# Part of the second head pair's key projection moved into the first stage of an encoder layer

## The chip, the cores and the metric

The kernel runs on one core of one Trainium2 chip. The metric is the device time of one execution in microseconds (us): shorter is better. The engines are named as in the profile: PE (TensorE, matrix multiplications and transposes), PEld (its weight loads), DVE (VectorE), ACT (ScalarE), POOL (GpSimd) and SP (SyncE, which issues the DMAs). Each engine works through its own list of instructions in order.

## What is computed

One encoder layer over 2048 tokens of width 1024, all in float32:

```
mod = silu(c) @ ada_w + ada_b                     # shift, scale, gate
h = layernorm(x) * (1 + scale) + shift
proj = h @ w_in                                   # 9216 columns
q_h, i_h, zf_fw, zf_bw, g_h, q_n, k_n, v_n, g_n = split(proj)
y_hg = bidirectional gated recurrence(q_h, i_h, zf_fw, zf_bw, g_h)
y_na = neighbourhood attention(q_n, k_n, v_n) * silu(g_n)   # 16 heads of 64
y = concat(y_hg, y_na) @ w_out
out = layernorm(2**0.25 * x + gate * y) * ln_g + ln_b
```

The change is in the projection `h @ w_in` for the keys of the attention.

## The kernel before

**Tokens and columns.** The kernel handles the tokens in two halves of 1024, and a half in two groups `g` of 512. `h` is kept transposed: 8 tiles `k` (128 of the 1024 channels each) of 128x512 for each group, every one of them as two float32r tiles, a rounded one and the remainder: `hts[g, k, 0]` (high) and `hts[g, k, 1]` (low). A weight is split the same way. A column tile is 128 columns of `w_in`; its projection for one group is 8 steps `k` of three matmuls each (weight high by h high, weight high by h low, weight low by h high), 24 matmuls of 128x512 that add up in one PSUM bank. `proj_mm` makes one step of three (L278). `evac` copies the bank out with ACT (L766) into a tile of the tag `raw`, which in this stage is one of eight buffers `e`.

**First stage** (`startup`, about the first 98 us). It normalizes the first 1024 tokens, computes shift and scale, and turns `x` into `h`, step by step over the list `order`: (0, 0) to (0, 7) for the first 512 tokens, then (1, 0) to (1, 7) for the second 512. For each step, PE does four transposes (`turn_`, L232), ACT adds scale and shift (L237) and makes the high part (L239), DVE the low part (L1211). Then `proj_mm` uses the step for three column tiles at once: keys, queries and gates of the attention's first head pair (PSUM banks `acc`). I call these nine matmuls a block. Behind each block `next(values)` does one step of the value projection (`vproj`, L291, twelve matmuls of 128x256; after its last step the copies L297). The turns run one step ahead: the loop body first issues the jobs of the step, then `turn_`, `high` and `low` of the next step, then the block. `jobs` puts the rest between: weight splits, `mod_sum` (a multiply and sum on DVE, L154, which gives shift and scale of one `k`), and for the second tokens `stat` (L202), `rates` (L180 to L209, with ACT's L182 and L183) and `scale` (ACT's L225 and DVE's L227, on `x` in place). For PE, SP, ACT and DVE the stage's instructions stand in the order in which the program writes them.

**The stream behind it.** `first_half` then goes through the eight head pairs of the attention for these 1024 tokens. While pair `w` is attended to (`natten_woven`: scores L1029 and L1036, softmax on DVE and ACT with L1045 to L1055, turns L1078, sums L1100), `first_stream` projects keys, queries and gates of pair `w + 1`, and `weave` mixes the two on PE by a table of costs: a step of three matmuls counts `KUS` = 0.68. Here only PE's order is the program's; a scheduler places the instructions of the others, and it also lets some of this stage's instructions into the end of the first stage (`Prep.k`, L966 to L968: copies of the keys into `KA`, `KB` and `KL`). Weights for the stream come through `Chunks`: `load` issues a DMA into one of four `wraw` buffers, `split` makes the two float32r tiles with ACT (L817) and DVE (L818).

`ps("po")` gives one of two PSUM banks, `tl("ada", ...)` one of four buffers of 128x2048, in which the modulation weights are loaded.

Of the kernel before, what the change touches and what calls it, by code (L numbers as in the profile page):

```python
# [11 lines left out]
F32R = mybir.dt.float32r  # L12
# [5 lines left out]
D = 1024  # L18
# [20 lines left out]
def body(ctx: ExitStack, tc: tile.TileContext, t):  # L39
# [234 lines left out]
    def proj_mm(pz, his, los, g, k):  # L274
        wh = his[k // 4][:, (k % 4) * P:(k % 4 + 1) * P]
        wl = los[k // 4][:, (k % 4) * P:(k % 4 + 1) * P]
        for n, (a, b) in enumerate(((wh, hts[g, k, 0]), (wh, hts[g, k, 1]), (wl, hts[g, k, 0]))):
            pe.matmul(pz, a, b, start=(k == 0 and n == 0), stop=(k == KT - 1 and n == 2))  # L278

    def vproj(src, dst, half, feed=None, fine=False):  # L280
        his, los = feed.take(4) if feed else load_split(lambda i: src[:, i * 512:(i + 1) * 512], 4)
        for t2 in range(2):
            pzs = [ps("pj"), ps("pj")]
            for k in range(KT):
                wh, wl = (w[k // 2][:, (k % 2) * 256:(k % 2 + 1) * 256] for w in (his, los))
                for tp in range(2):
                    for i in range(2):
                        g, o = divmod(((t2 * 2 + tp) * 2 + i) * P, GRP)
                        hh, hl = (hts[g, k, s][:, o:o + P] for s in range(2))
                        for n, (a, b) in enumerate(((hh, wh), (hh, wl), (hl, wh))):  # L290
                            pe.matmul(pzs[tp][:, i * 256:(i + 1) * 256], a, b, start=(k == 0 and n == 0 and i == 0), stop=(k == KT - 1 and n == 2), skip_group_check=True)  # L291
                if k % 2:
                    if k == KT - 1:
                        for tp, pz in enumerate(pzs):
                            v = tl("vo")
                            with tc.high_priority(offset=PRI):
                                act.activation(v, pz, AF.Copy)  # L297
# [553 lines left out]
    def first_stream(st, feed):  # L851

        if st.p % 2 == 0:
            for _ in vproj(t["w_v"][st.p // 2], nv_d[st.p // 2], 0, feed):
                feed.tick()
                yield 2.9
        todo = []
        for n, c in NCOL0:
            his, los = feed.take(2)
            for g in range(2):  # L860
                pz = ps("pj")
                for k in range(KT):
# [311 lines left out]
    def startup():  # L1174
# [29 lines left out]
        def turn_(g, k):  # L1204
            pts[g, k] = h_turn(xs[g], k)

        def high(g, k):
            tmps[g, k] = h_high(pts[g, k], k, hts[g, k, 0], True)

        def low(g, k):  # L1210
            dve.tensor_tensor(hts[g, k, 1], tmps[g, k], hts[g, k, 0], op=ALU.subtract)  # L1211
# [10 lines left out]
        for i in range(4):  # L1222
# [9 lines left out]
            (0, 3): [(mod_sum, 4), (w_split, 1, 1), (w_split, 2, 1)],  # L1232
            (0, 4): [(feed.split, 0), (mod_sum, 5)],
            (0, 5): [(mod_sum, 6), (stat, 1, 0), (feed.split, 0)],
            (0, 6): [(mod_sum, 7), (stat, 1, 1)],
            (0, 7): [(stat, 1, 2), (stat, 1, 3), (rates, 1), (scale, 1, 0, 2)],
            (1, 2): [(scale, 1, 1, 4)],
        }
# [8 lines left out]
        values = vproj(t["w_v"][0], nv_d[0], 0, feed, True)  # L1247
        rows = {n: [None, None] for n, _ in NCOL0}
        order = [(g, k) for g in range(2) for k in range(KT)]
        turn_(0, 0)  # L1250
        high(0, 0)
        w_split(0, 0)
        low(0, 0)
        for n, (g, k) in enumerate(order):
            for f, *a in jobs.get((g, k), []):
                f(*a)
            nxt = order[n + 1] if n + 1 < len(order) else None
            if nxt:
                turn_(*nxt)
            if nxt:  # L1260
                high(*nxt)
                low(*nxt)
            if (g, k) == (0, 7):
                feed.load(8)
                rp = bias_rows()
                bias_fill()
                dma(lg, t["lb_logits"])
                dma(normg, t["hg_norm_g"])
            if (g, k) == (1, 0):
                acc.update({(2, 1): ps("po"), (0, 1): ps("sc"), (1, 1): ps("sc")})  # L1270
                bias_tables(rp)
                bias_pair(0)
                dma(c_d.rearrange("(p k) -> p k", k=KT), mod["c8"])
            for i in (2, 0, 1) if g else (0, 1, 2):
                proj_mm(acc[i, g], *ws[i], g, k)
            if k == KT - 1:
                for i in range(3):
                    rows[NCOL0[i][0]][g] = evac(acc[i, g])
            next(values, None)
            if g:  # L1280
                feed.tick()
        return rows, feed

    def first_half(raws, feed):

        st = Prep(0, 0, raws)
        for n, g in (("k", 0), ("k", 1), ("q", 0), ("g", 0), ("q", 1), ("g", 1)):
# [90 lines left out]
    h_alloc()  # L1378
    with psum_phase("n0", NPS), tc.manual_schedule(engines={mybir.EngineType.PE}):
        with phase("st", SB_, SMS), tc.manual_schedule(engines={getattr(mybir.EngineType, e) for e in ("PE", "SP", "Activation", "DVE")}):  # L1380
            raws, feed = startup()
        with phase("n0", NB0, SM0):
            natten_init(4, 0)
            st = first_half(raws, feed)

    def reload(g):
        for k in range(KT):
# [251 lines left out]
```

## Time and profile before

| | us |
|---|---|
| median of 3 runs | 2625.78 (2624.72 to 2625.88) |
| profiled execution, its own time | 2628.06 |
| profiled execution, span of its instructions | 2626.3 |
| PE busy | 2562.5 (98%) |
| PEld busy | 2149.1 (82%) |
| DVE busy | 1738.8 (66%) |
| ACT busy | 1434.5 (55%) |

A timeline row reads: start, duration, engine, source line, operation, output<-input, count, and in brackets the idle time of the engine before it with what ended it. A row of stages reads: from:to, length, then busy us (and instructions) of PE, PEld, DVE, ACT and POOL, the granted TensorE clock as a share of the full one, the busy share of the DMA engines, and GB/s. Ends of matmuls are modelled; their starts are the better guide.

### The profile page before, as it was taken

What the parts mean: (1) busy time and instruction counts of PE and PEld (TensorE: products, weight loads), DVE (VectorE), ACT (ScalarE), POOL (GpSimd) and SP (SyncE); (2) the same over time, 40 slices, a digit from 0 to 9 for tenths busy, and PEclk for the clock granted to TensorE, in tenths of its full rate; (3) what the DMA queues carried; (4) which work ended last, traced back from release to release, by engine and by line L of the source; (5) the groups of instructions that cost most, each with busy time, mean ns of one, the idle gap of its engine ahead of it and who ended that gap; (6) DMA issues with size and microseconds to landing.
All of it is one profiled execution on the core that took longest, in us unless ns stands there. A gap on an engine that the chain in (4) does not pass through costs nothing.

```text
span 2626.3 us, 45803 instructions
## 1 busy us (share of the span) xinstructions
PE 2562.5 (98%) x17140; PEld 2149.1 (82%) x17140; DVE 1738.8 (66%) x4354; ACT 1434.5 (55%) x2856; POOL 108.7 (4%) x143
## 2 busy tenths in 40 slices
PE   6999999989999999999999999999999998999998
PEld 5888888878888888888888888888888886788887
DVE  7444545477777778877887787555777778558443
ACT  4534444366666566666766666454677777431110
POOL 0000000000000000000000000000000000042221
PEclk9999999999999999999999999999999999999999
DMA  7476454212111126212122222344455546443331
GB/s 272 141 212 143 133 169 154 93 48 71 65 64 58 65 69 219 84 52 78 65 64 67 74 75 75 109 144 129 122 143 139 147 133 172 125 153 129 97 97 57
DMA packets 225631, 295.87 MB, mean 113 GB/s; under 512 B 28807, under 2 KB 117511, under 8 KB 224263
## 3 DMA queue, kind: packets, MB, share of 16 engines
q1 hardware_dynamic: 225407, 292.93, 36.5%
q8 instruction: 135, 2.21, 0.4%
q14 instruction: 89, 0.73, 0.1%
HBM read 217.65 MB, written 66.99 MB: 108 GB/s over the span
## 4 chain that ended last, share of the span: by engine, by line
PE 72%; DVE 2%; DMA 2%; ACT 2%; issue 0%; DVEq 0%; SPq 0%; ACTq 0%
PE pj L278 39%; PE ps L1468 4%; PE ps L1469 4%; PE ps L1470 4%; PE pj L291 2%; PE ps L1100 2%; PE ps L1078 2%; PE ps L480 2%; PE ps L472 2%; PE ps L547 1%; PE ps L1029 1%; PE ps L571 1%; PE ps L573 1%; PE ps L519 1%; PE ps L645 1%; DMA bias<-tint 1%
## 5 line engine op out<-in xcount | busy, mean ns | idle before, releaser
L278 PE MATMUL pj<-h,wh 128*128 128x512 f32 x4000 | 1273.6, 399 | 4.2 <-ACT wh L817 1.9
L278 PEld LDWEIGHTS pj<-h,wh 128*128 128x128 f32 x4000 | 725.4, 188 | 156.4 <-issue 13.8
L278 PE MATMUL pj<-h,wl 128*128 128x512 f32 x2000 | 783.9, 392 | 0.0
L278 PEld LDWEIGHTS pj<-h,wl 128*128 128x128 f32 x2000 | 375.6, 188 | 83.4 <-DVE wl L793 0.4
L1050 ACT ACTIVATE pbuf<-pbuf,mx 128x480 f32<-128x480 f32 (+5 forms) x256 | 152.5, 597 | 116.5 <-DVE mx L1045 115.5
L291 PE MATMUL pj<-wh,h 128*128 128x256 f32 x1024 | 198.4, 288 | 4.1 <-ACT vt L297 3.8
L1045 DVE CUSTOM_DVE_ANT_1 pbuf<-ps,bias 128x480 f32<-128x480 f32 (+5 forms) x256 | 129.1, 540 | 110.0 <-PE ps L1036 46.7
L291 PEld LDWEIGHTS pj<-wh,h 128*128 128x128 f32 x1024 | 165.2, 194 | 7.9 <-ACT vt L297 4.5
L268 ACT ACTIVATE wh<-wr 128x512 fp32r<-128x512 f32 x192 | 120.3, 626 | 79.2 <-PE pj L278 68.9
L269 DVE TENSOR_TENSOR wl<-wr,wh 128x512 fp32r<-128x512 f32 x192 | 131.3, 684 | 48.1 <-ACT wh L268 47.9
L291 PE MATMUL pj<-wl,h 128*128 128x256 f32 x512 | 145.9, 285 | 0.0
L1084 ACT ACTIVATE pt<-ps 120x384 f32<-120x384 f32 (+3 forms) x128 | 65.2, 509 | 118.9 <-PE ps L1078 118.5
L1082 DVE COPY pt<-ps 120x384 f32<-120x384 f32 (+3 forms) x128 | 74.9, 585 | 66.0 <-PE ps L1078 65.0
L1078 PE MATMUL ps<-ident,pbuf 128*128 128x128 f32 (+2 forms) x832 | 113.7, 274 | 4.5 <-DVE pbuf L1055 3.4
L1078 PEld LDWEIGHTS ps<-ident,pbuf 128*128 128x128 f32 (+2 forms) x832 | 97.3, 137 | 22.8 <-ACT pbuf L1050 3.8
L466 DVE TENSOR_TENSOR de<-e,de 128x512 f32<-128x512 f32 x64 | 44.2, 691 | 94.4 <-ACT de L465 94.4
L1444 ACT ACTIVATE yh<-yr 128x512 fp32r<-128x512 f32 x52 | 32.7, 628 | 132.6 <-PE ps L1469 115.4
L766 ACT ACTIVATE e<-pj 128x512 f32<-128x512 f32 x98 | 58.3, 595 | 85.2 <-PE pj L278 78.0
L1055 DVE TENSOR_SCALAR pbuf<-pbuf,mx 128x480 f32<-128x480 f32 (+5 forms) x256 | 101.0, 412 | 3.9
L1517 DVE TENSOR_TENSOR vt<-ps,gt 128x512 f32<-128x512 f32 x24 | 16.5, 691 | 129.2 <-PE ps L1470 129.2
L291 PEld LDWEIGHTS pj<-wl,h 128*128 128x128 f32 x512 | 99.3, 194 | 1.4 <-issue 0.5
L447 DVE TENSOR_TENSOR_SCAN c<-c,g 128x128 f32<-128x128 f32 x256 | 88.4, 404 | 10.7 <-ACT c L437 10.7
(274 smaller groups left out, 4681.6 us busy)
## 6 DMA issues: line engine op xcount, KB each, us to landing
wr<-in_w_in SPq DMA_DIRECT2D x276, 256.0 KB
yr<-yq SPq DMA_DIRECT2D x64, 256.0 KB
bias<-tint SPq DMA_DIRECT2D x24, 480.0 KB
x<-in_x SPq DMA_DIRECT2D x32, 256.0 KB
ada<-in_ada_m SPq DMA_DIRECT2D x8, 1024.0 KB
wr<-in_w_v SPq DMA_DIRECT2D x32, 256.0 KB
nv<-vt SPq DMA_DIRECT2D x32, 256.0 KB
hs<-s SPq DMA_DIRECT2D x32, 256.0 KB
```

The lines of the kernel that those rows point to most:

```text
L268: act.activation(hi, raw, AF.Copy)
L269: dve.tensor_tensor(lo, raw, hi, op=ALU.subtract)
L278: pe.matmul(pz, a, b, start=(k == 0 and n == 0), stop=(k == KT - 1 and n == 2))
L291: pe.matmul(pzs[tp][:, i * 256:(i + 1) * 256], a, b, start=(k == 0 and n == 0 and i == 0), stop=(k == KT - 1 and n == 2), skip_group_check ...
L447: dve.tensor_tensor_scan(c[:, sl], c[:, sl], L[:, sl], 0.0, op0=ALU.add, op1=ALU.subtract)
L1045: return dve.tensor_tensor_reduce(s[:, 0:nk].rearrange("p (r c) -> p r c", c=kw), sc[:, 0:nk].rearrange("p (r c) -> p r c", c=kw), bt[:, 0 ...
L1050: act.activation(s[:, 0:nk], s[:, 0:nk], AF.Exp, scale=-1.0, bias=mx[:, 0:1], accum_out=mx[:, 1:2])
L1055: dve.tensor_scalar(s[:, 0:nk], s[:, 0:nk], mx[:, 2:3], 1.0, op0=ALU.mult, op1=ALU.mult)
L1078: pe.transpose(ptp[0:cw, c * P:(c + 1) * P], s[:, c * cw:(c + 1) * cw], ident)
L1468: pe.matmul(pz, yh[:, kk], wh, start=first, stop=False)
L1469: pe.matmul(pz, yh[:, kk], wl, start=False, stop=False)
L1470: pe.matmul(pz, yl[:, kk], wh, start=False, stop=last)
```

## The change

A fourth column tile, the keys of the second head pair, is projected for the first 512 tokens in the first stage. Its raw weights are loaded into the last two of the buffers `e` behind the loads that stood there, split with ACT's `fourth_split` (at step (0, 6)) and DVE's `fourth_low` (at step (0, 7)) into one of the `ada` buffers, and summed in the bank `ps("po")`. Its 24 matmuls stand in two parts: at (0, 7), 14 with the high weights ahead of the block, two more behind the value step, and the eight with the low weights behind the turns of (1, 0). At (0, 7) the block and its three copies `evac` now stand ahead of the step's jobs and of the next step's turns, and `vproj` has one more `yield`, so that its last copies come behind the eight matmuls. In the blocks of the last step each column tile is copied out right behind its own matmuls. `first_stream` for the second pair leaves out the column tile it is given, and the sum that `weave` spreads is `KT * KUS` less.

```diff
@@ vproj
                 if k % 2:
+                    if fine and k == KT - 1:
+                        yield None
                     if k == KT - 1:
@@ first_stream
             for g in range(2):
+                if st.raws[n][g]:
+                    todo = [(n, g)]
+                    continue
                 pz = ps("pj")
@@ startup
-            (0, 6): [(mod_sum, 7), (stat, 1, 1)],
+            (0, 6): [(lambda: fourth_split(),), (mod_sum, 7), (stat, 1, 1)],
...
+        fourth, fraw = ([], []), [tl("raw"), tl("raw")]
+        for a in range(2):
+            dma(fraw[a], t["w_in"][NCOL0[0][1] // P + 1][:, a * 512:(a + 1) * 512])
+
+        def fourth_split():
+            w = tl("ada", F32R, [P, 2 * D])
+            for a in range(2):
+                hi, lo = (w[:, o:o + 512] for o in (a * 512, D + a * 512))
+                act.activation(hi, fraw[a], AF.Copy)
+                fourth[0].append(hi)
+                fourth[1].append(lo)
+
+        def fourth_low():
+            for a in range(2):
+                dve.tensor_tensor(fourth[1][a], fraw[a], fourth[0][a], op=ALU.subtract)
+
+        def fourth_mm(pz, k, low):
+            wh, wl = (w[k // 4][:, (k % 4) * P:(k % 4 + 1) * P] for w in fourth)
+            for n, (a, b) in enumerate(((wl, hts[0, k, 0]),) if low else ((wh, hts[0, k, 0]), (wh, hts[0, k, 1]))):
+                pe.matmul(pz, a, b, start=(k + n + low == 0), stop=(low == 1 and k == KT - 1))
+
+        def block(g, k):
+            for i in (2, 0, 1) if g else (0, 1, 2):
+                proj_mm(acc[i, g], *ws[i], g, k)
+                if k == KT - 1:
+                    rows[NCOL0[i][0]][g] = evac(acc[i, g])
...
         for n, (g, k) in enumerate(order):
+            if (g, k) == (0, 7):
+                pz = ps("po")
+                for kx in range(KT - 1):
+                    fourth_mm(pz, kx, 0)
+                block(g, k)
             for f, *a in jobs.get((g, k), []):
                 f(*a)
             nxt = order[n + 1] if n + 1 < len(order) else None
-            if nxt:
-                turn_(*nxt)
-            if nxt:
-                high(*nxt)
-                low(*nxt)
+
+            def ahead():
+                if nxt:
+                    turn_(*nxt)
+                    high(*nxt)
+                    low(*nxt)
+
+            if (g, k) != (0, 7):
+                ahead()
...
-            for i in (2, 0, 1) if g else (0, 1, 2):
-                proj_mm(acc[i, g], *ws[i], g, k)
-            if k == KT - 1:
-                for i in range(3):
-                    rows[NCOL0[i][0]][g] = evac(acc[i, g])
-            next(values, None)
+            if (g, k) != (0, 7):
+                block(g, k)
+            if (g, k) == (0, 7):
+                next(values)
+                fourth_mm(pz, k, 0)
+                fourth_low()
+                ahead()
+                for kx in range(KT):
+                    fourth_mm(pz, kx, 1)
+                first = evac(pz)
+                next(values)
+            else:
+                next(values, None)
             if g:
                 feed.tick()
-        return rows, feed
+        for _ in values:
+            pass
+        return rows, feed, first
@@ first_half
+                if w == 0:
+                    nxt.raws["k"][0] = first
-                dense, total, steps = first_stream(nxt, feed), NLEN + (0 if w % 2 == 0 else VLEN), 8
+                dense, total, steps = first_stream(nxt, feed), NLEN + (0 if w % 2 == 0 else VLEN) - (0 if w else KT * KUS), 8
```

In the lists below, taken from the two built programs, names carry the number of their buffer: `ps_257` to `ps_259` are the banks of the block, `ps_554` is the fourth column tile's, `h_92` to `h_107` are the high and low parts of the first tokens' eight steps, `x_232` and its like are tiles of the second tokens, `e_...` the copies that `evac` makes. **PE around (0, 7), before:** the second tokens' turns, and behind them the block of (0, 7).

```order
L291 MATMUL pj_308<-wh_477,h_105 128x256
L232 MATMUL ps_571<-ident,x_232 128x128
L232 MATMUL ps_571<-ident,x_236 128x128
L232 MATMUL ps_571<-ident,x_245 128x128
L232 MATMUL ps_571<-ident,x_249 128x128
L278 MATMUL ps_257<-h_106,bk_359 128x512
L278 MATMUL ps_257<-h_107,bk_359 128x512
```

PE, now, from the end of the block's value step on:

```order
L291 MATMUL pj_312<-wh_481,h_107 128x256
L1274 MATMUL ps_554<-h_106,ada_515 128x512
L1274 MATMUL ps_554<-h_107,ada_515 128x512
L232 MATMUL ps_641<-ident,x_232 128x128
L232 MATMUL ps_641<-ident,x_236 128x128
L232 MATMUL ps_641<-ident,x_245 128x128
L232 MATMUL ps_641<-ident,x_249 128x128
L1274 MATMUL ps_554<-h_92,ada_515 128x512
L1274 MATMUL ps_554<-h_94,ada_515 128x512
```

The block and its value step have moved in front of these turns, with 16 of the 24 new matmuls; the last eight stand behind the turns. **ACT around (0, 7), before:** the rates and the scaling of the second tokens stand ahead of the copies of the block.

```order
L239 ACTIVATE h_106<-sg_522 128x512
L182 ACTIVATE l_558<-v_556 128x4
L183 ACTIVATE xr_555<-l_558 128x4
L225 ACTIVATE x_232<-x_232,xb_565,xr_555 128x512
L225 ACTIVATE x_236<-x_236,xb_565,xr_555 128x512
L237 ACTIVATE sg_576<-ps_571,shift,scale_85 128x512
L239 ACTIVATE h_108<-sg_576 128x512
L766 ACTIVATE e_606<-ps_257 128x512
```

ACT, now:

```order
L1263 ACTIVATE ada_515<-e_260 128x512
L1263 ACTIVATE ada_515<-e_261 128x512
L237 ACTIVATE sg_529<-ps_524,shift,scale_85 128x512
L239 ACTIVATE h_106<-sg_529 128x512
L768 ACTIVATE e_572<-ps_257 128x512
L768 ACTIVATE e_577<-ps_258 128x512
L768 ACTIVATE e_582<-ps_259 128x512
L182 ACTIVATE l_595<-v_593 128x4
L183 ACTIVATE xr_592<-l_595 128x4
L225 ACTIVATE x_232<-x_232,xb_602,xr_592 128x512
```

The two splits are new, and the block's three copies (L768 is the line of `evac` now) stand ahead of the rates. **ACT at (1, 7), the end of the stage, before:** between the two instructions that make `h` of that step stand the first pair's key copies and its gate.

```order
L237 ACTIVATE sg_853<-ps_848,shift,scale_85 128x512
L966 ACTIVATE KA_183_930<-e_606 64x512
L966 ACTIVATE KB_184_931<-e_606 64x512
L984 ACTIVATE sg_956<-e_610 128x512
L239 ACTIVATE h_122<-sg_853 128x512
```

ACT, now:

```order
L237 ACTIVATE sg_889<-ps_884,shift,scale_85 128x512
L971 ACTIVATE KA_185_960<-e_572 64x512
L971 ACTIVATE KB_186_961<-e_572 64x512
L989 ACTIVATE sg_986<-e_582 128x512
L971 ACTIVATE KA_188_963<-e_658 64x512
L971 ACTIVATE KB_189_964<-e_658 64x512
L239 ACTIVATE h_122<-sg_889 128x512
```

Two key copies of the second pair (from `e_658`, the fourth column tile) have come in there, out of the stream behind; DVE's two subtractions `KL` of theirs have moved ahead of the low part of `h` likewise.

More of the change, by code (lines that the diff above doesn't have):

```diff
@@ L1273, in startup, with first_half @@
                 dma(c_d.rearrange("(p k) -> p k", k=KT), mod["c8"])
-            for i in (2, 0, 1) if g else (0, 1, 2):
-                proj_mm(acc[i, g], *ws[i], g, k)
-            if k == KT - 1:
-                for i in range(3):
-                    rows[NCOL0[i][0]][g] = evac(acc[i, g])
-            next(values, None)
+            if (g, k) != (0, 7):
[11 more added lines that the diff above has]
+                next(values, None)
             if g:
                 feed.tick()
-        return rows, feed
-    def first_half(raws, feed):
+        for _ in values:
+            pass
+        return rows, feed, first
+    def first_half(raws, feed, first):
         st = Prep(0, 0, raws)
@@ L1380, in body @@
         with phase("st", SB_, SMS), tc.manual_schedule(engines={getattr(mybir.EngineType, e) for e in ("PE", "SP", "Activation", "DVE")}):
-            raws, feed = startup()
+            raws, feed, first = startup()
         with phase("n0", NB0, SM0):
             natten_init(4, 0)
-            st = first_half(raws, feed)
+            st = first_half(raws, feed, first)
     def reload(g):
```

## The prediction

> **What bounds the kernel now.** I read the page first, then PE's timeline of the first stage, then stages of it, then ACT and DVE around PE's long wait.
>
> ```profile
> span 2626.3 us, 45803 instructions
> PE 2562.5 (98%) x17140; PEld 2149.1 (82%) x17140; DVE 1738.8 (66%) x4354; ACT 1434.5 (55%) x2856; POOL 108.7 (4%) x143
> ```
>
> PE is busy for all but 64 us (2626.3 less 2562.5). The change takes no matmul away, it moves 24, so it can gain only where they fill some of those 64 us. PE's timeline around the step (0, 7) has the longest hole of the first stage:
>
> ```profile
> 52.32 0.28 PE L291 MATMUL pj<-wh,h 128*128 128x256 f32 x1
> 59.10 0.48 PE L232 MATMUL ps<-ident,x 128*128 128x128 f32 x1 [6.50 <-ACT x L225]
> 59.80 0.90 PE L232 MATMUL ps<-ident,x 128*128 128x128 f32 x3 [0.23 <-ACT x L225]
> 60.36 1.63 PE L278 MATMUL ps<-h,bk 128*128 128x512 f32 x3
> ...
> 63.65 0.28 PE L291 MATMUL pj<-wh,h 128*128 128x256 f32 x1
> ...
> 65.06 0.60 PE L232 MATMUL ps<-ident,x 128*128 128x128 f32 x4
> 65.42 0.71 PE L278 MATMUL ps<-h,vt 128*128 128x512 f32 x2
> ```
>
> PE waits 6.50 us for the scaling of the second tokens (L225), although the block of (0, 7) behind those transposes needs nothing of it. The stages (granted clock, DMA share and GB/s stand last) add two things:
>
> ```profile
> 39.00:44.00 5.00, 4.91 (x33) 4.22 (x31) 3.43 (x7) 1.93 (x3) 0.00 (x0) 1.00 0.96 382
> 44.00:48.00 4.00, 3.94 (x24) 3.40 (x24) 3.97 (x9) 1.41 (x2) 0.00 (x0) 1.00 0.04 16
> 52.40:59.10 6.70, 0.20 (x2) 0.00 (x1) 5.79 (x17) 1.85 (x5) 3.06 (x6) 0.77 0.46 161
> 59.10:63.60 4.50, 4.27 (x13) 3.37 (x14) 0.70 (x2) 2.99 (x5) 0.00 (x0) 0.59 0.01 4
> 100.00:140.00 40.00, 40.00 (x208) 32.28 (x206) 18.10 (x50) 17.89 (x40) 0.76 (x3) 1.00 0.60 174
> ```
>
> After the wait PE ran at a clock of 0.59, so the nine matmuls of the block took 3.29 us (60.36 to 63.65). And from 100 to 140, in the first head pair, where the 24 matmuls stand now, PE never waits.
>
> **Term 1, the stream: -5.4.** Matmuls of this kind at full clock:
>
> ```profile
> 100.77 0.61 PE L278 MATMUL pj<-h,wh 128*128 128x512 f32 x2
> ...
> 106.89 0.28 PE L1029 MATMUL ps<-KA,q 128*128 128x264 f32 x1
> ```
>
> Nine steps of three stand between these rows: 27 matmuls in 6.12 us, 0.227 each. Of 24, 5.44 us leave the first pair, whole if PE stays as full there as it is; what would spoil that is the first rival. [...]
>
> **Term 2, the hole: -1.4.** PE comes free at 52.32 + 0.12 = 52.44. It then has 14 new matmuls (3.18), the block (9 at 0.227: 2.04), the value step (63.65 to 65.06: 1.41) and two new ones (0.45), and is through at 59.52. Their inputs must be there, and the second tokens' chain must be followed through ACT:
>
> ```profile
> 51.53 0.78 ACT L237 ACTIVATE sg<-ps,shift,scale 128x512 f32<-128x512 f32 x1 [3.58 <-DVE scale L154]
> ...
> 56.77 0.20 ACT L182 ACTIVATE l<-v 128x4 f32<-128x4 f32 x1 [3.79 <-DVE v L180]
> ...
> 58.23 1.52 ACT L225 ACTIVATE x<-x,xb,xr 128x512 f32<-128x512 f32 x2 [1.02 <-DVE xb L209]
> 60.74 0.78 ACT L237 ACTIVATE sg<-ps,shift,scale 128x512 f32<-128x512 f32 x1 [0.99 <-PE ps L232]
> 61.55 0.63 ACT L239 ACTIVATE h<-sg 128x512 fp32r<-128x512 f32 x1
> ...
> 63.15 1.29 ACT L766 ACTIVATE e<-ps 128x512 f32<-128x512 f32 x2 [0.49 <-PE ps L278]
> ```
>
> - *The new splits* fit into the 3.58 us that ACT idles ahead of 51.53; two copies like L239 cost 1.3. Their weights are 0.5 MB more behind the loads: at 382 GB/s 1.4 us, and the queue is empty (16 GB/s) from 44 on. So they land by about 45.5. Cost nothing.
> - *The three copies ahead of the rates.* ACT copies a column tile as soon as PE has done it (the last row's wait), so the third one behind the modelled end of the block's last matmul (52.44 + 3.18 + 8 x 0.227 + 0.39 = 57.83; a single one is shown for 0.61 - 0.227 = 0.39), and ACT is through with it, in 0.6, at about 58.4. L182 then starts 1.65 later than at 56.77. This is the price of moving the block ahead of the jobs: DVE's steps of the rates, the scaling and the turns behind it all wait for that, +1.65.
> - *The turns* follow L225 by 0.87 and 1.57 (58.23 to 59.10 and 59.80). L225 now starts at 59.88, the turns at 60.75 and 61.45, and PE has waited 1.2 instead of 6.5. They end at about 61.8.
> - *The eight low matmuls* (1.82) run until 63.6 and the next turns (0.36) until 64.0. That covers what the block covered before: L237 and L239 need 1.44 from the end of the turns, so the high part is there at 63.4. The low part on DVE follows 0.03 behind and takes 0.69:
>
> ```profile
> 62.21 0.69 DVE L1211 TENSOR_TENSOR h<-sg,h 128x512 fp32r<-128x512 f32 x1 [3.10 <-ACT h L239]
> ```
>
> It is there at 64.1, just when the second matmul of block (1, 0) wants it (64.2). DVE's two subtractions of the new tile (2 x 0.69) come behind its scaling, before PE's first low matmul of `k` 4.
>
> Block (1, 0) so starts at 64.0 and not at 65.42: -1.4, with all 24 matmuls done. Most of this comes from the clock: the 1.25 us that the block lost at 0.59. Bounds: -1.7 (copies done a little sooner) and +1.5 (the clock falls again, second rival).
>
> **Term 3, the end of the stage: +1.3.** Two key copies of the second pair now stand on ACT ahead of `h` of (1, 7):
>
> ```profile
> 90.75 0.76 ACT L237 ACTIVATE sg<-ps,shift,scale 128x512 f32<-128x512 f32 x1
> 91.41 0.62 ACT L966 ACTIVATE KA<-e 64x512 fp32r<-64x512 f32 x1
> 92.05 0.63 ACT L966 ACTIVATE KB<-e 64x512 fp32r<-64x512 f32 x1
> ...
> 93.24 0.62 ACT L239 ACTIVATE h<-sg 128x512 fp32r<-128x512 f32 x1
> ```
> ```profile
> 93.89 0.69 DVE L1211 TENSOR_TENSOR h<-sg,h 128x512 fp32r<-128x512 f32 x1
> ```
> ```profile
> 94.64 0.50 PE L278 MATMUL ps<-h,vt 128*128 128x512 f32 x1 [0.23 <-DVE h L1211]
> ```
>
> Before, PE already waited 0.23 for the low part. The copies come 0.64 apart, so two more make the high and the low part 1.3 later, and nothing hides that. The bounds are 0.6 (if ACT comes to them sooner against PE) and 1.5. They leave the stream behind, where they cost nothing.
>
> **Term 4, the last copies: -0.4.** PE then waits for the value copies L297, which stand on ACT behind the block's three copies:
>
> ```profile
> 95.90 0.85 PE L278 MATMUL ps<-h,q 128*128 128x512 f32 x3
> ...
> 99.28 0.73 PE L278 MATMUL pj<-h,wh 128*128 128x512 f32 x2 [1.10 <-ACT vt L297]
> ```
> ```profile
> 96.10 1.78 ACT L766 ACTIVATE e<-ps 128x512 f32<-128x512 f32 x3 [0.84 <-PE ps L278]
> ...
> 98.63 1.08 ACT L297 ACTIVATE vt<-pj 128x512 f32<-128x512 f32 x2
> ```
>
> Now each column tile is copied right behind its own matmuls. The last one ends 0.6 behind the end of the third column at 96.75, so at 97.4 and not at 97.88. Some 0.4 of the 1.10 goes (bounds 0 and 0.5).
>
> The loads, the feed's last split (one place later than before, its chunk is wanted 5 us on), and the moved stores lie beside a full PE. Far behind, a few rows of ACT, DVE and SP swap neighbours; I give them nothing, with 0.5 either way.
>
> **Sum:** -5.4 - 1.4 + 1.3 - 0.4 = -5.9. The profiled execution took 2628.06 (span 2626.3 and 1.8 around it), 2.3 above the median of the runs; it would take 2622.2, and the median 2625.8 becomes 2619.9. About 0.2% (5.3 us) is what a measurement of this kernel can tell from no change, so the gain is just beyond it.
>
> **Rivals.** *First, the first pair gives it back.* It loses 24 of its dense matmuls, and its softmax, splits and loads are no shorter. Between the scores of a block and the turns of its shares there were 42 dense matmuls, now 33 (7.5 us). For it: SP issues loads without a pause there. Against it:
>
> ```profile
> 118.11 0.82 PE L1078 MATMUL ps<-ident,pbuf 128*96 128x128 f32 x6
> ...
> 139.00 0.28 PE L1029 MATMUL ps<-KA,q 128*128 128x264 f32 x1
> ```
> ```profile
> 109.59 0.36 DVE L1055 TENSOR_SCALAR pbuf<-pbuf,mx 128x264 f32<-128x264 f32 x1
> ```
> ```profile
> 124.05 0.51 SPq L727 DMA_DIRECT2D bias<-tedge  x1
> ```
>
> The shares were done at 109.95, the turns came at 118.11: 8 us of slack, of which 2 go. The second pair's bias was issued at 124.05 for scores at 139.00; of those 15 us 5.4 go, and 2 for its later place. Given back whole, the sum is -0.5 and the time 2625.3; half of it, 2622.6. Chance 0.24.
>
> *Second, the clock.* PE still waits 1.2 us, and a wait can let the clock fall. The nearest rows are two waits later on, and the stage behind the second:
>
> ```profile
> 278.11 0.73 PE L278 MATMUL pj<-h,wh 128*128 128x512 f32 x2 [1.90 <-ACT wh L817]
> ```
> ```profile
> 2207.04 1.50 PE L1078 MATMUL ps<-ident,pbuf 128*120 128x128 f32 x6 [3.41 <-DVE pbuf L1055]
> ```
> ```profile
> 2207.00:2209.00 2.00, 1.96 (x8) 1.89 (x9) 1.78 (x7) 1.77 (x5) 0.00 (x0) 0.50 0.77 245
> ```
>
> Behind 1.90 us two matmuls took what they took at 99.28, behind 3.41 the clock was 0.50. So it decides somewhere between, with turns 0.7 to 2.2 later than I put them. Then the 4.5 us behind them run at half rate: 2.2 us more, with the 0.7 a sum of -3.0 and 2622.8. Chance 0.08.
>
> *Third, slower: ACT held by the new load.* ACT is in order, and at (0, 6) it now waits for the new weights. If these land behind 51.5, `h` of (0, 7), the rates and the scaling all slip by the rest. It decides from 51.5; the gain is gone at 57.4, and at 62.7 the kernel is slower by 0.2%. It would take a queue that other transfers hold; the row from 44 to 48 speaks against it. A landing at 64 gives 2632.4. Chance 0.06.
>
> That the change does not do what it says is not open: the order of the built program shows the 24 matmuls moved.
>
> **The numbers.** My forecast has 0.60, its own range 2618.4 to 2620.5, all of it faster by over 0.2%. The first two rivals lie within 0.2%, 0.32 together; the third is the slower side, with 0.02 for what I don't see. So faster 0.60, same 0.32, slower 0.08. The range takes in the forecast's lower bound (-7.4, from -5.4, -1.7, +0.6, -0.5 and the swaps' -0.4) and reaches up to most of the first rival: 2618.4 to 2624.4.
>
> **What would show it.** PE's wait in front of the second tokens' turns falls from 6.50 to about 1.2, the granted clock from there to 64 is near 1, and block (1, 0) starts near 64.0. PE waits 1.2 to 1.5 in block (1, 7). The stream's first matmul comes near 98.8 (term 2 to 4: -0.5) and the second pair's first scores near 133.1. New waits of PE between 99 and 134 would make the first rival right; a wait of ACT ahead of the new splits the third; a wait over 2 us at the turns, my reckoning of the copies wrong.

## The result, and the profile after

The changed kernel took 2617.18 us, the median of 7 runs (2616.25 to 2622.09). Its ratio to the kernel before is 0.9969, with a 95% interval of 0.9957 to 0.9981. That is faster by more than the 0.2% which the prediction set as the bound, and 1.2 us below the lower end of its range (2618.4). Three later rounds of the same kernel gave medians of 2618.82, 2619.12 and 2617.73. All its 32 runs have a mean of 2618.90 (standard error 0.33), the 84 runs of the kernel before beside them 2626.09 (0.19). So the change is worth -7.2 us with an error of 0.4, where -5.9 was forecast.

The page of the changed kernel, its head:

```profile
span 2615.3 us, 45806 instructions
PE 2559.9 (98%) x17140; PEld 2146.8 (82%) x17140; DVE 1738.2 (66%) x4356; ACT 1435.5 (55%) x2858; POOL 108.4 (4%) x143
```

PE has the same 17140 matmuls, its idle time fell from 63.8 to 55.4 us and its busy time by 2.6. The span is 11.0 shorter in this pair of profiles, more than any comparison of times shows; why is told under Repeats. PE's timeline around the step (0, 7), where 6.50 us of waiting stood before, then at the end of the stage and the beginning of the stream, at the second pair's first scores (L1034), and at two later waits:

```profile
52.35 3.36 PE L1274 MATMUL ps<-h,ada 128*128 128x512 f32 x14
55.55 0.84 PE L278 MATMUL ps<-h,bk 128*128 128x512 f32 x3
...
59.02 0.63 PE L1274 MATMUL ps<-h,ada 128*128 128x512 f32 x2
60.61 0.33 PE L232 MATMUL ps<-ident,x 128*128 128x128 f32 x1 [0.96 <-ACT x L225]
61.31 0.55 PE L232 MATMUL ps<-ident,x 128*128 128x128 f32 x3 [0.38 <-ACT x L225]
61.62 2.11 PE L1274 MATMUL ps<-h,ada 128*128 128x512 f32 x8
63.91 0.71 PE L278 MATMUL ps<-h,vt 128*128 128x512 f32 x2
...
93.68 0.50 PE L278 MATMUL ps<-h,vt 128*128 128x512 f32 x1 [1.10 <-ACT h L239]
94.54 0.50 PE L278 MATMUL ps<-h,vt 128*128 128x512 f32 x1 [0.36 <-DVE h L1216]
98.69 0.73 PE L278 MATMUL pj<-h,wh 128*128 128x512 f32 x2 [0.62 <-ACT vt L299]
...
133.02 0.28 PE L1034 MATMUL ps<-KA,q 128*128 128x264 f32 x1
...
272.11 0.73 PE L278 MATMUL pj<-h,wh 128*128 128x512 f32 x2 [1.90 <-ACT wh L819]
...
557.73 2.05 PE L482 MATMUL ps<-v,ke 128*128 128x128 f32 x8 [8.15 <-DVE Sf L493]
```

The block and 16 of the 24 new matmuls (L1274) fill what was the hole; the turns wait 0.96 + 0.38 = 1.34 us, and the last eight new ones stand behind them. Block (1, 0) starts at 63.91, not 65.42. The wait in block (1, 7) has grown from 0.23 to 1.46, and that of the stream's first matmul has shrunk from 1.10 to 0.62. The second pair's first scores stood at 139.00 before and have moved by 5.98. The last two rows are two waits that both kernels have; their ends are milestones. The first, ahead of the fifth pair's projection, stood at 278.11 before and has moved by 6.00, the second by 6.04. Its row before:

```profile
563.77 2.05 PE L480 MATMUL ps<-v,ke 128*128 128x128 f32 x8 [8.14 <-DVE Sf L491]
```

ACT in the same place:

```profile
47.75 1.13 ACT L1263 ACTIVATE ada<-e 128x512 fp32r<-128x512 f32 x2
51.42 0.78 ACT L237 ACTIVATE sg<-ps,shift,scale 128x512 f32<-128x512 f32 x1 [2.53 <-DVE scale L154]
...
56.43 1.96 ACT L768 ACTIVATE e<-ps 128x512 f32<-128x512 f32 x3 [3.57 <-PE ps L278]
58.28 0.20 ACT L182 ACTIVATE l<-v 128x4 f32<-128x4 f32 x1
...
59.74 1.52 ACT L225 ACTIVATE x<-x,xb,xr 128x512 f32<-128x512 f32 x2 [1.02 <-DVE xb L209]
```

The two new splits run at 47.75 and wait for no load. The three copies of the block hold the rates (L182) until 58.28, 1.51 later than before. The granted clock of the 12 us from 58 to 70, in the kernel before, then in two profiles of the changed one (busy time of PE, PEld, DVE, ACT and POOL, then the clock, DMA share and GB/s):

```profile
58.00:70.00 12.00, 10.67 (x57) 9.25 (x58) 3.76 (x10) 7.45 (x12) 0.00 (x0) 0.80 0.17 57
```
```profile
58.00:70.00 12.00, 10.67 (x62) 8.89 (x62) 5.99 (x17) 7.91 (x14) 0.25 (x1) 1.00 0.26 80
```
```profile
58.00:70.00 12.00, 10.66 (x64) 8.94 (x63) 5.63 (x16) 8.19 (x15) 0.25 (x1) 1.00 0.23 75
```

With 1.34 us of waiting the clock stays at 1.00. It does so in all four profiles of the changed kernel, and in six of the kernel before it was 0.71 to 0.85.

### The profile page after: what moved, and what is told of

Its sections match the earlier page's. It is cut to its first block, busy times and chain, and to the rows that moved or that the text cites. A ratio compares the mean times of both kernels' runs of the same rounds, so it can differ in the third digit from the quotient of the medians.

```text
span 2615.3 us, 45806 instructions
## 1 busy us (share of the span) xinstructions
PE 2559.9 (98%) x17140; PEld 2146.8 (82%) x17140; DVE 1738.2 (66%) x4356; ACT 1435.5 (55%) x2858; POOL 108.4 (4%) x143
## 4 chain that ended last, share of the span: by engine, by line
PE 74%; DVE 2%; ACT 1%; DMA 1%; issue 0%; DVEq 0%; ACTq 0%; SPq 0%
PE pj L278 40%; PE ps L1520 4%; PE ps L1521 4%; PE ps L1522 4%; PE ps L1105 3%; PE pj L291 2%; PE ps L1083 2%; PE ps L482 2%; PE ps L474 2%; PE ps L549 1%; PE ps L1034 1%; PE ps L573 1%; PE ps L575 1%; PE ps L521 1%; PE ps L647 1%; PE ps L1041 1%
## 5 line engine op out<-in xcount | busy, mean ns | idle before, releaser
L278 PE MATMUL pj<-h,wh 128*128 128x512 f32 x3984 | 1267.8, 399 | 3.7 <-ACT wh L819 1.9
L278 PEld LDWEIGHTS pj<-h,wh 128*128 128x128 f32 x3984 | 721.6, 188 | 155.4 <-issue 13.9
L278 PE MATMUL pj<-h,wl 128*128 128x512 f32 x1992 | 780.5, 392 | 0.0
L278 PEld LDWEIGHTS pj<-h,wl 128*128 128x128 f32 x1992 | 373.8, 188 | 82.9 <-DVE wl L820 0.4
L768 ACT ACTIVATE e<-pj 128x512 f32<-128x512 f32 x97 | 57.8, 596 | 85.2 <-PE pj L278 78.5
```

## The experiments

The theory: the gain is the sum of the four terms, all of it made ahead of 280 us. The rivals: it comes partly from the swapped rows far behind; or PE's saved clock carries it, and the 24 matmuls matter little. Each edit is made on the changed kernel. Where only the stage is meant, lengths are counted from the first matmul of the first projection (L278, at about 19 us, since what lies ahead of it varies by some tenths) to the stream's first matmul.

**Repeats.** Both kernels again, unchanged, for the spread of each stretch.

> The kernel before, unchanged, profiled a second time. Open is why the profiled spans lie 11.0 us apart (2626.3 and 2615.3) when the first stage gives 6.0: between 564 and 2240 us of the first profile the kernel before waits 4.7 us more. Theory A, chance: these waits end at transfers that land late now and then; the second profile shows the wait of 3.41 us ahead of the last pair's turns, and those of 0.90, 0.38 and 0.31 us, at other lengths though no instruction differs, and its span moves by over 1 us from 2626.3. Theory B, a fixed effect of the change far behind the stage: the four waits come back within 0.2 us and the span within 0.5.

> The changed kernel, unchanged, profiled a second time. By A its late waits (0.26, 0, 0, 1.52 us at the four places) come out otherwise too, in either direction, and the median lies between 2616 and 2621. By B they come back within 0.2 us. Both expect the first stage as in the first profile: block (1,0) at 63.9, the stream's first matmul at 98.7, within 0.1.

> The changed kernel a third time. Open is whether the surplus over the forecast (7.4 between the medians of 15 and 25 runs, against 5.9) is chance. Chance: the far part, from the end of the 8.15 us wait near 558 us to the end, took 2062.5 and 2059.6 us in two profiles of before, 2057.6 and 2061.2 in two of after; a third falls between 2056 and 2063, with the transfer waits and the clock's low stretches at other places, and the mean over all runs moves towards 2619.9. A fixed effect: the mean stays 7.5 under before.

> The changed kernel a fourth time, beside the others of this round: by the forecast's sum and the mean of before (2626.1 over 68 runs) 2620.2, by the mean of its own 26 runs 2619.0. [...]

> The kernel before, unchanged, a third profile (of six). Behind the wait of 8.15 us near 563 us the mean of 84 runs of before is 2.2 us longer than that of 32 runs of after, though the far part has the same instructions. If that is a fixed place, the profiles of before are longer there than the nine of the kernels with the moved tile, whose far part is the same (ends 0 to 4.7 us over the shortest, mean 1.7): the candidates are the store that the rows at about 1664 us wait for, and the load ahead of the last pair's turns near 2207 us. If it is chance, the far parts of before fall between the same ends.

> The kernel before, unchanged, a fourth profile, for the spread of its far part: a fixed place is longer than in the nine profiles with the moved tile each time, chance hits one place or another.

> The kernel before, unchanged, a fifth profile, for the spread of its far part: a fixed place is longer than in the nine profiles with the moved tile each time, chance hits one place or another.

> The kernel before, unchanged, a sixth profile, for the spread of its far part: a fixed place is longer than in the nine profiles with the moved tile each time, chance hits one place or another.

The times: the kernel before again 2625.87 (ratio to itself 0.9997, 0.9988 to 1.0006), and in four single profiles 2624.53, 2625.73, 2625.78 and 2623.22; the changed one 2618.82 (0.9972, 0.9961 to 0.9982), 2619.12 (0.9977, 0.9968 to 0.9985) and 2617.73 (0.9970, 0.9959 to 0.9982). Its first ratio, 0.9969, was no outlier, but its first median was the lowest of four. Three stretches of ten profiles, in us:

| | before, six profiles | changed, four profiles |
|---|---|---|
| first projection matmul to stream | 79.97, 79.70, 80.17, 81.19, 80.63, 79.82 | 79.51, 79.54, 79.53, 79.49 |
| end of the wait of 8.15 us | 563.77, 562.84, 564.94, 565.79, 565.74, 563.12 | 557.73, 557.75, 559.95, 557.85 |
| from there to the end, beside the first changed profile | 4.96, 2.02, 0.26, 0.54, 0.72, 0.78 | 0, 3.67, -0.31, 4.62 |

Up to the milestone the change is worth 564.37 - 558.32 = 6.05. Counted from the first projection matmul, as the first row is, the milestone comes after 545.46 in the mean of the six and 539.02 in that of the four: 6.44. In the first profile of each it is 544.46 and 538.54, which is 5.92. The rest of the program, the same work in both, differs by up to 5 us between two executions of *one* kernel, and its means (1.55 and 2.00) say nothing for or against the swapped rows. The kernel before was by chance profiled in its longest one: 11.0 between the two profiles is 6.04 of the change and 4.96 of that.

Of the 4.96, 3.2 come at one place, the last pair's turns. PE, in a repeat of the kernel before, then in the first and a later profile of the changed one (the prediction quotes 3.41 for the first profile of before):

```profile
2202.25 0.84 PE L1078 MATMUL ps<-ident,pbuf 128*120 128x128 f32 x6 [1.30 <-DVE pbuf L1055]
```
```profile
2196.99 0.84 PE L1083 MATMUL ps<-ident,pbuf 128*120 128x128 f32 x6 [1.52 <-DVE pbuf L1060]
```
```profile
2199.55 1.48 PE L1083 MATMUL ps<-ident,pbuf 128*120 128x128 f32 x6 [2.94 <-DVE pbuf L1060]
```

The same wait is 1.30 in one execution of before and 3.41 in another, 1.52 and 2.94 in two of the changed kernel. Behind the long ones the six turns take 1.48 or 1.50, behind the short ones 0.84: the granted clock is 0.50 behind the 3.41 (2207 to 2209 us in the first profile of before) and 1.00 behind the 1.52 (2197 to 2199 in the first of the changed kernel). The chain behind it begins at SP and ends in a wait of ACT for a weight load of the output projection, here in the first profile of before and of after:

```profile
2188.75 0.36 SPq L1111 DMA_DIRECT2D yq<-vt  x1
...
2197.56 0.34 SPq L1423 DMA_DIRECT2D vt<-in_w_out  x1
...
2200.98 0.63 ACT L1428 ACTIVATE wo<-vt 128x512 fp32r<-128x512 f32 x1 [3.17 <-DMA vt<-in_w_out]
```
```profile
2180.60 0.36 SPq L1116 DMA_DIRECT2D yq<-vt  x1
...
2187.64 0.34 SPq L1475 DMA_DIRECT2D vt<-in_w_out  x1
...
2190.94 0.63 ACT L1480 ACTIVATE wo<-vt 128x512 fp32r<-128x512 f32 x1 [1.29 <-DMA vt<-in_w_out]
```

The load is issued 8.8 us behind the store in the one and 7.0 in the other, in the same order, and ACT waits 3.17 or 1.29 for it.

**wo3_late: take that wait away.** One split of those weights moves a place back.

```diff
-    extra = {..., 8: [(wo_split, 0, 2, 3), (wo_load, 0, 6, 7)],
-             9: [(wo_split, 0, 4, 5)], ...
+    extra = {..., 8: [(wo_split, 0, 2), (wo_load, 0, 6, 7)],
+             9: [(wo_split, 0, 4, 5, 3)], ...
```

> The changed kernel with one split of the output weights (row block 3) issued after those of blocks 4 and 5 in the last pair. In all profiles so far PE waits 1.3 to 3.4 us ahead of the last pair's turns, and ACT waits there for this block's load, which itself waits for the store of an earlier result out of the same buffer to land. If the variable landing of that store is what makes the far part vary there, this wait falls under 0.5 us, no low clock follows it, and the time is 1 to 3 us under after. If something else holds PE there, the wait stays at 1.3 to 3 us.

```profile
2197.51 0.84 PE L1083 MATMUL ps<-ident,pbuf 128*120 128x128 f32 x6 [0.69 <-DVE pbuf L1060]
```

PE's wait fell to 0.69, but the time is 2619.33 (0.9979, 0.9970 to 0.9988), no better than the changed kernel beside it on the same chip (0.9977). The wait is one of several places where executions part, and taking the one away didn't make them agree: these eleven runs spread from 2614.75 to 2626.48.

**rates_first: the block where it stood, between the rates and the scaling.** It undoes the price on ACT, and keeps the 24 matmuls.

```diff
-            (0, 7): [(stat, 1, 2), (stat, 1, 3), (rates, 1), (scale, 1, 0, 2)],
+            (0, 7): [(stat, 1, 2), (stat, 1, 3), (rates, 1),
+                     (lambda: block(0, 7),), (scale, 1, 0, 2)],
...
-                block(g, k)
```

> In block (0,7) the rates of the second tokens are issued ahead of the block's three copies on ACT, so that the copies fall into the time in which DVE works out the bias, and the scaling follows them. By the trace of after the scaling then starts 1.3 us earlier (58.4 for 59.7 us), the two waits of PE for the scaled tokens (0.96 and 0.38 us) go, block (1,0) starts at 62.6, and the time is 1.3 us under after, 2615.9. Rival: the copies come later and hold the accumulators' banks or the first turn's ACT work, and PE waits there instead: 0 to 0.5 us over after.

ACT of this kernel, then PE:

```profile
56.12 0.21 ACT L182 ACTIVATE l<-v 128x4 f32<-128x4 f32 x1 [3.80 <-DVE v L180]
56.47 1.55 ACT L768 ACTIVATE e<-ps 128x512 f32<-128x512 f32 x3
57.91 1.53 ACT L225 ACTIVATE x<-x,xb,xr 128x512 f32<-128x512 f32 x2
```
```profile
59.48 0.55 PE L232 MATMUL ps<-ident,x 128*128 128x128 f32 x3 [0.27 <-ACT x L225]
...
62.07 0.72 PE L278 MATMUL ps<-h,vt 128*128 128x512 f32 x2
...
96.86 0.72 PE L278 MATMUL pj<-h,wh 128*128 128x512 f32 x2 [0.62 <-ACT vt L299]
```

The first projection matmul stands at 18.68 in this profile and at 19.19 in the changed kernel's. Counted from it, the rates start 1.65 sooner, block (1, 0) starts 1.33 sooner, and the stage takes 78.18, 1.33 less. PE waits 0.27 at the turns. The time: 2617.23 (0.9966, 0.9954 to 0.9979), a mean of 2617.71 with an error of 0.70.

**keys_late: the second pair's two key copies stay in the stream.**

```diff
-            keep = pinned if src in self.bk else lambda x: x
+            keep = pinned if src in self.bk or (self.p, self.half, i) == (1, 0, 0) else lambda x: x
```

> The two copies of the second pair's keys are kept in program order on ACT, and so fall behind the last copies of the stage instead of ahead of h of the last block. By the forecast's third term (loss of 1.3) h of block (1,7) is ready 1.3 us earlier, PE's waits of 1.10 and 0.36 us there go, and the stream's first matmul stands 78.2 us behind the first projection matmul, where after has 79.5. If the stage's gain lasts to the end, the time is 1.3 under after; if the clock or the late transfers swallow it, the stage shows it and the time does not. Rival: the second pair's keys are late for its first scores, with a wait on PE near 132 us.

```profile
92.64 0.50 PE L278 MATMUL ps<-h,vt 128*128 128x512 f32 x1 [0.23 <-DVE h L1216]
...
96.80 0.73 PE L278 MATMUL pj<-h,wh 128*128 128x512 f32 x2 [0.62 <-ACT vt L299]
```

The waits of 1.10 and 0.36 in block (1, 7) become the 0.23 of before, and the stage takes 78.04, 1.5 less. Term 3 was these two copies. The time: 2617.48 (0.9972, 0.9961 to 0.9983), mean 2618.32, error 0.68.

**both: the two edits together**, in two rounds.

> Rates ahead of the three copies, and the key copies behind the stage, together. By the two stage traces the terms add: the stream's first matmul 76.9 us behind the first projection matmul (after 79.5, rates first 78.2), and 2.6 us under after where nothing swallows it. By the rival that the program's far part decides between runs, the stage shows 2.6 and the median of five rounds lies anywhere from 4 under after to 1 over.

> Rates first and keys late together, a second time, for its mean: the stage gave 2.7 us more than after in the trace (first stream matmul 76.8 us behind the first projection matmul for 79.5), the first seven runs' mean 0.6 (2618.4 for 2619.0). If the stage's gain lasts, the mean over all rounds goes to 2616.4; if the far part eats it, it stays at 2618.4.

```profile
91.67 0.50 PE L278 MATMUL ps<-h,vt 128*128 128x512 f32 x1 [0.23 <-DVE h L1216]
...
95.83 0.73 PE L278 MATMUL pj<-h,wh 128*128 128x512 f32 x2 [0.62 <-ACT vt L299]
```

The stage takes 76.79 and 76.75 in two profiles, 2.7 less than in the changed kernel: the two prices add. The times are 2617.73 (0.9973, 0.9962 to 0.9983) and 2616.59 (0.9963, 0.9950 to 0.9975). The mean of the 12 runs is 2617.71, error 0.56: 8.4 below the kernel before, level with rates_first alone (2617.71), and 1.2 below the changed one with an error of 0.65. So the lead is not separated from none, and of the 2.7 only 1.2 shows in the time; why is not shown.

**twice: the 24 matmuls stay in the stream as well.** The stage computes the new tile, but the first pair's stream computes that column again and nothing uses the tile. Terms 2 to 4 act alone.

```diff
-                if w == 0:
-                    nxt.raws["k"][0] = first
-                dense, total, steps = ..., NLEN + (...) - (0 if w else KT * KUS), 8
+                dense, total, steps = ..., NLEN + (...), 8
```

> The fourth tile is computed in the first stage and its result left unused; the second pair's stream computes it again as before. By the terms of the forecast: the 24 matmuls stay in the stream (nothing of the 5.4), the two key copies go back behind it (nothing of the loss of 1.3), and what is left is the hole (1.4) and the last copies (0.4): 1.8 under the kernel before, 2624.0, and the stream's first matmul at about 97.4. If the 2.6 us by which the medians beat the forecast are a fixed effect of the moved start far behind, it is 4.4 under the kernel before, 2621.4. A third reading, that the stream's tile is worth more than its 24 matmuls, gives 2624.0 here and puts the whole surplus on that tile.

> The fourth tile computed twice, a second time. Its first profile kept the 1.8 us of the stage up to the stream and then lost 2.7 us that before did not: a wait of 0.62 us with 0.71 of low clock near 253 us and a low clock after the 1.90 us wait near 275 us (2.10 for 0.74). If that was chance, the position of the wait near 558 us, counted from the first projection matmul, is 542.5 now (545.1 then, 544.2 and 544.5 in before) and the mean moves towards 2624.3. If it comes with the kernel, both come back and the mean stays near 2625.9.

Its stage takes 78.12 and 78.08, 1.85 less than in the first profile of before, as the terms say. The times don't show that: 2626.29 (0.9999, 0.9990 to 1.0008) and 2625.06 (0.9998, 0.9989 to 1.0007), together -0.1 with an error of 0.5. In both profiles the far part is long, by 4.35 and 6.91, and 3.3 of that come at one place, near 1716 us, in both. A store there, its issue on SP in the repeat of the kernel before and what waited for it on ACT, then PE:

```profile
1714.64 0.33 SPq L360 DMA_DIRECT2D yq<-t  x1
...
1716.72 0.63 ACT L343 ACTIVATE t<-t 128x512 f32<-128x512 f32 x1 [0.62 <-DMA yq<-t]
...
1718.17 0.39 PE L352 MATMUL ps<-rh,ones 128*128 128x512 f32 x1
```

The same in the two profiles of twice (the issue in the first, the waits in the second and the first):

```profile
1715.68 0.33 SPq L362 DMA_DIRECT2D yq<-t  x1
...
1720.72 0.49 PE L354 MATMUL ps<-rh,ones 128*128 128x512 f32 x1 [1.35 <-DVE rh L347]
```
```profile
1718.50 0.63 ACT L345 ACTIVATE t<-t 128x512 f32<-128x512 f32 x1 [2.60 <-DMA yq<-t]
...
1719.64 0.51 PE L354 MATMUL ps<-rh,ones 128*128 128x512 f32 x1 [1.51 <-DVE rh L347]
```

ACT waits 2.60 for the store's buffer instead of 0.62, and PE, which waited for nothing, now waits 1.35 or 1.51. The granted clock is then 0.50 for 3.41 us, from 1722.00 in the first profile and from 1720.66 in the second. The DMA queues while that store was under way (packets, MB, share of the 16 engines), in before and in twice:

```profile
q1 hardware_dynamic: 144, 0.26, 33.2%
```
```profile
q1 hardware_dynamic: 144, 0.26, 18.0%
q8 instruction: 1, 0.02, 2.1%
```

In twice one packet of the instruction queue falls among the store's 144 and the store lands after 3.81 us (3.97 in the second profile), not 2.00. Both profiles have it at the same place, and in the sixteen other profiles the store there lands after 1.99 to 2.02; whose packet it is, and why it comes there, was not shown. It is a second price of this experiment, so its time says little on terms 2 to 4, and the stage's length is what counts.

**no_tile: the 24 matmuls nowhere.** The tile is left out of the stage too, and the second pair's first key column is taken from another raw tile: the time without this work, and not the reference's output.

```diff
-                    fourth_mm(pz, kx, 0)
...
-                fourth_mm(pz, k, 0)
...
-                for kx in range(KT):
-                    fourth_mm(pz, kx, 1)
-                first = evac(pz)
+                first = rows["k"][0]
```

> The changed kernel without the fourth tile's 24 matmuls: they are neither in the first stage nor in the stream (left out: the second pair's keys of the first tokens; the first pair's stand in their place). It prices what the tile costs inside the stage. If it is free there, as the forecast has it, PE waits 4.5 to 5 us for the scaled tokens where it now works, block (1,0) starts within 0.3 us of after's (44.7 us behind the first projection matmul), and the time is that of after, up to 1.3 us more where the clock falls after the longer wait. If the tile's work in the stage costs something, block (1,0) comes earlier by that much and the time falls under after.

PE, and the granted clock behind the turns:

```profile
58.72 0.33 PE L232 MATMUL ps<-ident,x 128*128 128x128 f32 x1 [1.81 <-ACT x L225]
...
61.50 1.52 PE L278 MATMUL ps<-h,vt 128*128 128x512 f32 x2 [1.07 <-ACT h L239]
```
```profile
58.00:70.00 12.00, 9.83 (x41) 7.87 (x42) 4.69 (x12) 6.46 (x10) 0.25 (x1) 0.72 0.43 110
```

The expectation of the waits did not come true. PE waits 1.81, 0.38 and 1.07, together 3.26 and not 4.5 to 5, because the block and its copies come sooner, and with them the rates (by 1.63) and the scaling. Block (1, 0) starts 42.58 us behind the first projection matmul, 2.14 before that of the changed kernel (44.72), where 0.3 was the most that a free tile allowed. But the granted clock is 0.50 from 60.26 to 67.08, and at its end the stage is not shorter: 80.09, against 79.5 with the matmuls. So the tile's work delays block (1, 0) by 2.1 us, and costs the stage nothing on balance, since the clock stays at 1.00 with it. The time, 2617.58 (0.9966, 0.9953 to 0.9978), is 1.4 below the changed kernel's mean. The error is 0.4 by the spread of its own five runs (0.6), and 0.9 if one run has the usual 1.8, so it may be chance; its stage doesn't explain it, nor does its profile's far part (0.20).

## Why the prediction was right, and where it was not

- **Term 1, the stream, -5.4: right.** The second pair's first scores moved by 5.98 (139.00 to 133.02) and the stream's first matmul by 0.59 (99.28 to 98.69), so the first pair is 5.39 shorter. PE has no wait in it, before or now: the first rival fell. So the matmuls that left the stream carry most of the gain, and the saved clock of the stage does not.
- **Term 2, the hole, -1.4: right**, -1.51 by the rows, of which 0.12 is the lead ahead of the first projection matmul (19.31 and 19.19), so -1.39, and by the steps given: 1.34 of waiting at the turns (1.2 forecast), copies done near 58.3 (58.4), L225 at 59.74 (59.88). That the copies ahead of the rates have a price is shown by rates_first.
- **Term 3, +1.3: right**, 0.23 to 1.46 in block (1, 7), and the two copies alone by keys_late.
- **Term 4, -0.4: right**, 1.10 to 0.62.
- **Third rival: fell.** The splits wait for no load.
- **Second rival: did not occur, but its reading was wrong.** "So it decides somewhere between" 1.90 and 3.41 took one row with the clock up behind 1.90 us for a rule. In nine of the eighteen profiles the same wait is followed by a low clock (last section), so its length alone does not tell, and for a wait near 1.34 us one execution's rows could not bound the rival.
- **The step that failed: "Far behind, a few rows of ACT, DVE and SP swap neighbours; I give them nothing, with 0.5 either way."** That nothing is their mean price, no run contradicts. The 0.5 was wrong: it is meant for the swaps, while the 2000 us behind the change vary by up to 5 us between executions of one kernel. One run has a standard deviation of about 1.8 us, and a median of seven one of about 0.9 us. The range's lower end came from the terms' bounds in one execution and had no room for that, so a gain of 5.9 by the trace and a first median 8.6 below could both be. With it, the range should have reached about 1 us lower. That the first median was the lowest of four is chance: of the three later ones 2618.82 and 2619.12 lie inside the range, and so does the mean of all 32 runs, 2618.90.
- **Beside it, one trace stood for the mean.** The first pair of profiles gives 5.92 from the first projection matmul to the milestone, as forecast, the means of six and four 6.44. In the first profile of the kernel before the stage was 0.3 shorter than in the mean of six, and the clock stayed up behind the wait of 1.90 us, which it did in three of six. So this trace undersold what the clock costs the kernel before.
- **Still open:** the 32 runs give -7.2 with an error of 0.4, the profiles up to the milestone -6.44 with an error of about 0.7. The difference of 0.8 is within these errors; no place for it was found, and the swapped rows far behind are not excluded as a part of it.

## What to carry to other kernels

A change that fills a wait is worth its matmuls where they leave a full stretch, plus the clock that the wait had cost, minus each instruction that it pushes ahead of the waiting chain: the three were read from rows here to some 0.1 us each. Before giving a range, take the spread of the *untouched* rest of the program from the runs shown, since a forecast for a median of a few runs can't be narrower than that. And when two profiles differ by more than the times do, align them stretch by stretch before explaining the rest.

## What was unexpected of the hardware

**The same wait was followed by a full clock in some executions and by a low one in others.** PE's wait of 1.90 us ahead of the fifth pair's projection is the same in all eighteen profiles. Behind it the clock was low in nine of them, the kernel before in three of its six. Four us of the first profile of before, 1.5 us behind the wait's end, then those of a repeat of the same kernel:

```profile
279.60:283.60 4.00, 4.00 (x19) 2.99 (x18) 1.94 (x7) 1.59 (x5) 0.25 (x1) 1.00 0.66 218
```
```profile
279.50:283.50 4.00, 4.00 (x15) 2.95 (x14) 1.23 (x4) 0.30 (x1) 0.00 (x0) 0.75 0.66 212
```

Nineteen matmuls in the one, fifteen in the other, at clocks of 1.00 and 0.75; behind the same wait it was 0.57 in rates_first (271.8 to 275.8 us) and 0.59 in twice (278.3 to 282.3). From the stream's first matmul to the milestone the three low profiles of before take 1.3 to 1.6 us longer than the other three. In the trace's records of the granted clock, the first profile of before steps up at 25.27, 62.82 and 2209.80 us: 37.55 and 2146.98 apart, 11 and 629 times 3.4133, the length of its shortest stretch at one clock, which ends at 2209.80. In all eighteen traces each stretch at one clock, but for the last that the profile's end cuts off, is a multiple of it: in the first profile of before eleven stretches of 3.41 to 1181.01 us, in that of the changed kernel seven of 6.83 to 1181.01. Why is not shown.

The multiples tell the two halves apart. Counted on in steps of 3.4133 us from a step of the clock in the same trace, the wait ended 0.04 to 1.17 us behind a multiple in the nine profiles whose clock stayed up (0.25 in the first of before, 1.17 in the first of the changed kernel); in the nine others it ended 1.78 to 3.35 us behind one, and the clock fell at the next. The two ranges lie apart, but no run moves this wait by itself, so that its place decides is the author's reading. How long a wait has to be is not shown: up to 1.86 of the 1.90 us lay between two multiples without a fall, and 1.78 were followed by one. Nor is it shown that the 1.34 us of the changed kernel can never cost the clock.

**Some stores landed late with a packet of the instruction queue among their own.** In the eighteen profiles 108 of the 256 KB stores of this kind had the DMA engines to themselves and landed after 1.99 to 2.02 us. Four had one packet of the instruction queue beside their own 144 and nothing else, all in the two profiles of twice: 2.50, 2.57, 3.81 and 3.97. In the one of 3.81 the packet held its engine for 1.35 us, from 1.00 us behind the issue. Not all stores with such a packet were late: of eleven more stores that had such a packet and at most eight packets of other transfers beside them, ten landed after 2.00 to 2.15 and one after 3.06.
